# Second MLP of a hybrid decoder: seven products in all pairs of the seventh phase, its sums spread over the last phase, the last group of products in two halves

## The chip, the cores and the metric

The kernel runs on one core of one Trainium2 chip. The metric is the time of one execution on the device in microseconds (us); less is better. TensorE (PE) multiplies, VectorE (DVE) and ScalarE (ACT) work on tiles, GpSimd (POOL) and SyncE (SP) mostly issue DMA transfers. Each engine takes its own instructions in a fixed order; semaphores tie the engines together.

## The reference, cut to what matters

The reference is two layers of a decoder on 256 tokens and 16 leading meta tokens, width 2048, in float32: an RWKV-7 mixer, an MLP, a gated linear attention (GLA) with 4 heads, and a second MLP, each behind an RMS norm and added to its input. At the end stands a final RMS norm with a gain, and the meta tokens are dropped.

```
def rms_norm(x, g, eps=NORM_EPS):
    y = xf * lax.rsqrt(jnp.mean(xf * xf, axis=-1, keepdims=True) + eps)
    return y * g

def sq_relu_mlp(x, w1, w2):
    h = jax.nn.relu(x @ w1)
    return (h * h) @ w2          # w1: 2048 x 8192, w2: 8192 x 2048
```

The change concerns the second MLP's product with w2, the sum of that product with the residual, and the final norm. Other parts of the program are touched only where they prepare data for it.

## The kernel before, in words

The span has five stages, one after the other: the RWKV mixer (to some 592 us), the first MLP (function `mlp`, to some 1305), the GLA (`gla`, to some 1690), its output product, and the second MLP (`mlp1`, to the end at 2337).

**Weights.** TensorE works on float32 numbers as pairs of reduced-precision parts. A weight tile is loaded as `raw` by SyncE's queue; ScalarE casts it to `hi` (line 149 or 664), VectorE subtracts to get `lo` (line 150, or line 372 by way of the helper `tt`), and TensorE makes three matmuls of each product: with hi, with lo, with hi (lines 498 to 500 in `mlp1`; 172 to 174 in the other stages).

**The second MLP.** The 8192 hidden units are cut into 4 blocks b of 16 rows of 128; two rows make a pair p. The product with w2 is made in units (b, g, p), where g is a half of the 2048 outputs. `PHASES` gives the order of the eight phases (b, g); a phase has 8 pairs. The hidden rows of the next block (`row`, the product with w1, 16 ordinary matmuls for each of two stream entries) are woven between the pairs, except in the last phase.

An ordinary pair is a 2 by 2 block product with 8 products (24 matmuls of 128 x 512) from two weight tiles. A "fast" pair is the same product in Winograd's form with 7 products (21 matmuls) from three weight tiles A, B and E and a half tile G, which VectorE makes by subtracting a half of B from a half of A (`raw4`, in `split`, behind the lo of B). The slots A, B, E and G write PSUM banks 1 and 2, 6 and 7, 5 and 3, and 4. `FAST = [8, 8, 8, 4]` says how many pairs of each block are fast: all eight in blocks 0 to 2, four in block 3. Fast pairs use hidden blocks `HS` in 7 combinations (128 x 128 each, made by `sums` and `halves`), ordinary ones 4.

After a stretch of phases that share g, the banks are emptied and combined into `htok`, the residual in token layout: plain sums (`add`) and scaled sums (`into`, line 493), spread over later slots by `later(slot, f)`. The list `rest` has those for a stretch in which all pairs are fast (`alone`). The four steps on banks that ScalarE empties (`nc.scalar.mul`, `nc.scalar.copy`) are put behind the casts of their slot.

**The last phase**, (3, 1), takes its pairs in the order 0, 1, 4, 2, 3, 5, 6, 7: four fast ones, four ordinary ones. In phase (3, 0) of before, pairs 0 to 3 are fast and 4 to 7 ordinary, and its sums go to the first slots of the last phase. The last two pairs "close": the two products of token half 1 (banks 2 and 3) are made first, then its norm; then the 12 matmuls of one product of half 0 (`spare`, bank 0), then the 12 of the other (bank 4), then the norm of half 0. `final` squares a quarter of a token half and sums it (line 479), `most` adds these sums, `norm` makes the scale by two activations (lines 606, 607), scales (612, 613) and stores. `gain(t)` multiplies half the outputs of token half t by the gain `nf` ahead of that.

**What sets the order.** `mlp1` runs under a manual schedule on PE, DVE, ACT and SP: the order is that of the loop at its end. At stream entry i it issues what `later` put there (`before`), then the cast and the lo of entries up to four tiles ahead (`SETS = 4`), then what `later` put behind the casts (`behind`), then the matmuls of entry i. There are five raw buffers, and two more from three entries behind the last row. GpSimd is not under that schedule.

**The differences.** Fast pairs need differences of w2's quarters (tile `diff` in DRAM). `differences` makes them ahead of the second MLP, one unit (b, g, p) at a time: `fetch` (line 344: three loads of 256 KB by GpSimd's queue), `form` (lines 350 to 352: three VectorE operations, behind a small GpSimd copy in line 349), `store` (line 358). A step forms the unit fetched `delay` steps earlier, and stores the one before. `ticks` spreads the steps over rows of a stage. The first `EARLY = 52` units are made in the first MLP, with delay 2, the other 4 in the GLA, with delay 1, over 12 products: in the GLA the steps are at the ends of products 2, 4, 6, 8, 10 and 12, six products in each head.

## Time and profile before

| | us |
|---|---|
| median of 3 runs | 2339.42 |
| lowest and highest | 2338.92, 2340.03 |
| the profiled execution | 2338.97 |
| its span (first to last instruction) | 2337.2 |
| TensorE busy | 2308.0 (99% of the span) |
| VectorE busy | 1816.0 (78%) |
| ScalarE busy | 1378.0 (59%) |
| GpSimd busy | 301.4 (13%) |

A row of a timeline reads: start in us, duration in us, engine, line, operation, out<-in by the program's names, then the shape; `xN` is the number of instructions that the row stands for. In square brackets stands how long the engine was idle before it, and what released it. Matmuls are pipelined, so a row's duration is longer than the distance to the next one; the distance is the price. A tile is named by its first letters: `lo`, `hi`, `raw`, `HS`, `htok`; PSUM banks are `pu` (1, 2), `pt` (7, 6), `pm` (5), `pry` (3) and `pj` (4, 0).

### The profile page before, as it was taken

The page shows a single profiled execution, that of the slowest core. Times are in us where ns is not written, and L with a number is a line of the kernel's source. Part 1 is how long each engine was busy: PE and PEld are TensorE (multiplying, and loading weights), DVE is VectorE, ACT ScalarE, POOL GpSimd, SP SyncE. Part 2 cuts the span into 40 slices and gives each one's busy share as a digit, 9 for nine tenths or more (in the row PEclk, how much of TensorE's full clock was granted, in tenths as well). Part 3 has the DMA queues.
Part 4 walks back from the last instruction along what each step waited for, and adds up shares of the span by engine and source line. Part 5 has one row for each costly group of instructions (what it writes and reads, how often), then busy time and mean ns, then how long its engine had stood idle before and what let it go on. Part 6 is the DMA issues. An engine that isn't in the chain of part 4 may idle for free.

```text
span 2337.2 us, 49049 instructions
## 1 busy us (share of the span) xinstructions
PE 2308.0 (99%) x19183; PEld 2175.8 (93%) x19183; DVE 1816.0 (78%) x2979; ACT 1378.0 (59%) x2167; POOL 301.4 (13%) x597
## 2 busy tenths in 40 slices
PE   9999999999999999999999999999999999999998
PEld 8888888889999999999999999999998888898987
DVE  8868986848677667767767787677768989989877
ACT  6488645556555445445445565455577777777766
POOL 0000000000144444444430011000000000000000
PEclk9999999999999999999999999999999999999999
DMA  6459754535799999999996665555557777877875
GB/s 213 161 193 310 246 169 141 153 90 172 257 314 334 314 318 325 325 323 320 330 319 227 198 227 199 175 174 182 209 196 263 272 271 265 274 266 265 274 267 188
DMA packets 200326, 567.75 MB, mean 243 GB/s; under 512 B 41184, under 2 KB 56800, under 8 KB 199968
## 3 DMA queue, kind: packets, MB, share of 16 engines
q1 hardware_dynamic: 173216, 476.53, 59.7%
q0 software_dynamic: 26880, 88.10, 12.1%
q8 instruction: 151, 2.47, 0.4%
q14 instruction: 79, 0.65, 0.1%
HBM read 504.38 MB, written 58.46 MB: 241 GB/s over the span
## 4 chain that ended last, share of the span: by engine, by line
PE 83%; DVE 10%; ACT 3%; issue 2%; DMA 1%; SPq 0%; DVEq 0%; ACTq 0%
PE pj L172 16%; PE pj L174 16%; PE pj L173 16%; PE pj L418 10%; PE pj L419 5%; PE pj L205 2%; DVE lo L150 2%; PE pj L206 1%; PE pu L498 1%; PE pu L500 1%; PE pu L499 1%; PE pt L500 1%; PE pt L498 1%; PE pt L499 1%; ACT hi L149 1%
## 5 line engine op out<-in xcount | busy, mean ns | idle before, releaser
L149 ACT CAST hi<-raw 128x1024 fp32r<-128x1024 f32 (+1 forms) x562 | 526.1, 947 | 593.9 <-PE pj L173 530.6
L150 DVE TENSOR_TENSOR lo<-raw,hi 128x1024 fp32r<-128x1024 f32 (+1 forms) x562 | 613.1, 1100 | 224.8 <-ACT hi L149 220.1
L172 PE MATMUL pj<-x,hi 128*128 128x272 f32 (+1 forms) x2560 | 728.4, 285 | 2.0 <-DVE r L703 0.9
L174 PE MATMUL pj<-x,lo 128*128 128x272 f32 (+1 forms) x2560 | 714.7, 279 | 4.4 <-DVE lo L150 4.1
L173 PE MATMUL pj<-x,hi 128*128 128x272 f32 (+1 forms) x2560 | 713.6, 279 | 0.0
L172 PEld LDWEIGHTS pj<-x,hi 128*128 128x128 f32 x2560 | 484.8, 189 | 14.8 <-issue 6.5
L174 PEld LDWEIGHTS pj<-x,lo 128*128 128x128 f32 x2560 | 484.9, 189 | 6.8 <-DVE lo L150 6.5
L173 PEld LDWEIGHTS pj<-x,hi 128*128 128x128 f32 x2560 | 485.0, 189 | 2.5 <-issue 1.4
L372 DVE TENSOR_TENSOR lo<-raw,hi 128x1024 fp32r<-128x1024 f32 x364 | 405.1, 1140 | 72.1 <-ACT hi L664 70.8
L664 ACT CAST hi<-raw 128x1024 fp32r<-128x1024 f32 x364 | 352.3, 981 | 112.6 <-PE pj L418 30.7
L418 PE MATMUL pj<-x,hi 128*128 128x512 f32 x1024 | 339.5, 383 | 0.0
L172 PE MATMUL pj<-h,hi 128*128 128x272 f32 x1024 | 285.7, 279 | 0.0
L173 PE MATMUL pj<-h,hi 128*128 128x272 f32 x1024 | 285.7, 279 | 0.0
L174 PE MATMUL pj<-h,lo 128*128 128x272 f32 x1024 | 285.7, 279 | 0.0
L419 PE MATMUL pj<-x,lo 128*128 128x256 f32 x1024 | 279.2, 273 | 0.0
L418 PEld LDWEIGHTS pj<-x,hi 128*128 128x128 f32 x1024 | 193.5, 189 | 26.7
L419 PEld LDWEIGHTS pj<-x,lo 128*128 128x128 f32 x1024 | 196.4, 192 | 1.9 <-DVE lo L372 0.2
L172 PEld LDWEIGHTS pj<-h,hi 128*128 128x128 f32 x1024 | 193.5, 189 | 0.0
L173 PEld LDWEIGHTS pj<-h,hi 128*128 128x128 f32 x1024 | 193.5, 189 | 0.0
L174 PEld LDWEIGHTS pj<-h,lo 128*128 128x128 f32 x1024 | 193.5, 189 | 0.0
L358 POOL DMA_DIRECT2D diff<-x x168 | 90.2, 543 | 14.3 <-DVE x L351 5.1
L344 POOL DMA_DIRECT2D x<-w_d x168 | 89.8, 540 | 0.3
(359 smaller groups left out, 3517.7 us busy)
## 6 DMA issues: line engine op xcount, KB each, us to landing
raw<-mlp_w_d SPq DMA_DIRECT2D x384, 512.0 KB, 6.1
raw<-gla_in_d SPq DMA_DIRECT2D x98, 512.0 KB, 3.3
x<-w_d POOLq DMA_DIRECT2D x168, 256.0 KB, 6.8
diff<-x POOLq DMA_DIRECT2D x168, 256.0 KB, 8.6
raw<-w_rkv_d SPq DMA_DIRECT2D x80, 512.0 KB, 3.9
raw<-w_d SPq DMA_DIRECT2D x69, 512.0 KB, 4.5
raw<-diff SPq DMA_DIRECT2D x55, 512.0 KB, 5.2
raw<-gla_o_d SPq DMA_DIRECT2D x32, 512.0 KB, 3.3
```

Source lines behind the costliest of these rows:

```text
L149: nc.scalar.copy(hi[:, h], raw[:, h])
L150: nc.vector.tensor_tensor(out=lo[:, h], in0=raw[:, h], in1=hi[:, h].bitcast(F32), op=ALU.subtract)
L172: nc.tensor.matmul(out, hi[:, ws], xh, start=first, stop=False)
L173: nc.tensor.matmul(out, hi[:, ws], xl, start=False, stop=False)
L174: nc.tensor.matmul(out, lo[:, ws], xh, start=False, stop=last)
L205: nc.tensor.matmul(wide, hi[:, ws], xt, start=kt == 0, stop=False)
L344: nc.gpsimd.dma_start(x[:, body], w[:, k])
L358: nc.gpsimd.dma_start(self.diff[b, g, i][:, k], x[:, body])
L372: tt = lambda o, a, b, op: nc.vector.tensor_tensor(out=o, in0=a, in1=b, op=op)
L418: nc.tensor.matmul(wide, hi[:, ws], xt, start=kt == 0, stop=False)
L419: nc.tensor.matmul(narrow, lo[:, ws], xt[:, 0], start=False, stop=kt == KT - 1)
L664: nc.scalar.copy(hi, raw)
```

## The change

`FAST` becomes a table by phase: phase (3, 0) has eight fast pairs, phase (3, 1) still four. So 60 units need differences instead of 56, of which 54 are made in the first MLP and 6 in the GLA. Pairs 4 to 7 of block 3 are now fast in one phase and ordinary in the other; the one hidden block that only the ordinary form needs goes to a tile `X`. The sums of phase (3, 0) are those of an `alone` stretch, and `rest` is put at slots 8 to 14 behind its last tile, with the squares behind them. `gain(0)` moves from the ordinary pairs of the last phase to behind the norm of token half 1. The last product is made as two halves of 256 columns, in banks 4 and 1, with a squared sum for each half. The load of `nf` moves from SyncE's queue early in phase (3, 0) to GpSimd's queue at entry 12 of the last phase. `raw4` and `fsq` have one buffer instead of two.

```diff
-FAST = [8, 8, 8, 4]
+FAST = {phase: 8 for phase in PHASES}
+FAST[3, 1] = 4
 
-EARLY = 52
+EARLY = 54
...
-                if p >= FAST[b]:
-                    halves(slot + 1 + wait, F[:, :4], 0, 4)
-                    return
+                if p >= FAST[b, 1]:
+                    fourths[p] = X = self.t(hp, [P, 2, P], "X", KT // 2 - FAST[3, 1], F32R)
+                    later(slot + 2 + wait, lambda: nc.scalar.copy(X[:, 0], x21), True)
+                    later(slot + 3 + wait, lambda: tt(X[:, 1], x21, X[:, 0].bitcast(F32), ALU.subtract))
...
                                 for n, f in enumerate(rest):
-                                    later(slot + 7 + 2 * n, f)
+                                    later(slot + (7 + 2 * n if b < NHB - 1 else (8, 10, 10, 11, 11, 12, 14)[n]), f)
+                                if b == NHB - 1:
+                                    for n in range(4):
+                                        later(slot + 16 - n // 2 * 4, lambda n=n: final(n // 2, n % 2))
...
-                        if end and p == FAST[b] and k == 0:
-                            later(slot + 1, lambda: gain(0))
                         for at in (2, 3, 4, spare):
...
                         norm(1)
-                        for at in (spare, 4):
-                            for n, (X, m, pair) in enumerate(closing):
-                                h, ws = places[at][2:]
-                                product(at, (X[:, 0, 2 * m + h], X[:, 1, 2 * m + h]), pair, ws, False, n == 3)
-                            empty(at)
-                            if at == spare:
-                                most(0)
+                        gain(0)
+                        h, ws = places[spare][2:]
+                        for n, (X, pair) in enumerate(closing):
+                            product(spare, X[h], pair, ws, False, n == 3)
+                        empty(spare)
+                        most(0, (0, 1, 3))
+                        h, ws = places[4][2:]
+                        for i, at in enumerate((4, 1)):
+                            for n, (X, pair) in enumerate(closing):
+                                product(at, X[h], pair, ws, i == 1 and n == 0, n == 3, slice(P * i, P * i + P))
+                            into(0, 0, own[at], slice(SEQ * i, 512))
+                            final(0, 2 * g, i)
+                            if i == 0:
+                                add(sum3[:, :1], sum3[:, :1], ssq[:, 0, 4:])
+                                mean(0)
                         norm(0)
...
-            if n == len(PHASES) - 2:
-                gains_at = len(stream)
+            if n == len(PHASES) - 1:
+                gains_at = len(stream) + 12
...
-                    nc.sync.dma_start(nf, ap["nf"].to_broadcast([P, D]))
+                    nc.gpsimd.dma_start(nf, ap["nf"].to_broadcast([P, D]))
```

The order of instructions at three places follows, on VectorE; numbers behind a name are those of its buffer. Lines are those of each kernel, so that line 372 of before is 373 of the change. First the passage from phase (3, 0) to the last phase; `lo` is a weight tile's low part, `raw_4…` a half tile, `hres_72` the place of the sums u2, u3 and so on, `htok` the residual. Before:

```order
L372 TENSOR_TENSOR lo_28574<-raw_28468,hi_28573 128x1024
L372 TENSOR_TENSOR lo_28590<-raw_28488,hi_28589 128x1024
L372 TENSOR_TENSOR raw_4451_28593<-raw_28468,raw_28488 128x512
L372 TENSOR_TENSOR lo_28613<-raw_28506,hi_28612 128x1024
L372 TENSOR_TENSOR lo_4458_28619<-raw_4451_28593,hi_4457_28618 128x512
L372 TENSOR_TENSOR lo_28640<-raw_28529,hi_28639 128x1024
L493 SCALAR_TENSOR_TENSOR htok_22567<-pm_22575,rs_3273_22570,htok_22567 128x512
L372 TENSOR_TENSOR lo_28652<-raw_28555,hi_28651 128x1024
```

And with the change, at the first fast pair of the last phase as well:

```order
L373 TENSOR_TENSOR lo_28704<-raw_28596,hi_28703 128x1024
L373 TENSOR_TENSOR lo_28722<-raw_28621,hi_28721 128x1024
L373 TENSOR_TENSOR raw_4487_28725<-raw_28596,raw_28621 128x512
L373 TENSOR_TENSOR hres_72<-pt_22632,hres_72 128x512
L373 TENSOR_TENSOR hres_72<-pt_22631,hres_72 128x512
L373 TENSOR_TENSOR lo_28741<-raw_28672,hi_28740 128x1024
L373 TENSOR_TENSOR lo_4494_28747<-raw_4487_28725,hi_4493_28746 128x512
L373 TENSOR_TENSOR lo_28758<-raw_28675,hi_28757 128x1024
L373 TENSOR_TENSOR hres_72<-pm_22633,hres_72 128x512
L496 SCALAR_TENSOR_TENSOR htok_22625<-pm_22633,rs_3279_22628,htok_22625 128x512
L373 TENSOR_TENSOR lo_28775<-raw_28691,hi_28774 128x1024
```

Three plain sums, two of them from banks 6 and 7 (`pt`), now stand between the weight tiles of the first fast pairs, beside the scaled sum from bank 5 (`pm`) that stood there before.

Second, GLA's first head, at the end of its first product of values; `vs` is that product, `Am` a score block, `x` a unit of w2 that is formed, `lo` the next weight tile. What an instruction waits for stands in brackets; DMASW are GpSimd's transfers. Before:

```order
L1491 TENSOR_TENSOR vs_18026<-pj_17965,acc_17543 128x272 [waits PE_49]
L1491 TENSOR_TENSOR Am_18033<-pt_18028,gc_17552 80x256 [waits PE_49]
L150 TENSOR_TENSOR lo_18197<-raw_18194,hi_18196 128x1024 [waits DMAHW2_49,Activation_49]
L1491 TENSOR_TENSOR A_17960<-Am_18033,A_17960 80x256 [waits Activation_49]
L1491 TENSOR_TENSOR Am_18044<-pt_18037,gc_17552 128x192 [waits PE_49]
L1491 TENSOR_TENSOR Am_18051<-pt_18048,gc_17552 128x64 [waits DVE_49,PE_49]
```

And with the change:

```order
L1500 TENSOR_TENSOR vs_18058<-pj_17997,acc_17575 128x272 [waits PE_49]
L351 TENSOR_TENSOR x_17720<-x_17720,x_17719 128x513 [waits DMASW6_49,DMASW5_49,Pool_49]
L151 TENSOR_TENSOR lo_18229<-raw_18226,hi_18228 128x1024 [waits DMAHW2_49,Activation_49]
L352 TENSOR_TENSOR x_17719<-x_17719,x_17718 128x512 [waits DMASW4_49,DVE_49]
L1500 TENSOR_TENSOR Am_18075<-pt_18070,gc_17584 80x256 [waits PE_49]
L353 TENSOR_TENSOR x_17718<-x_17718,x_17720 128x512 [waits DVE_49]
L1500 TENSOR_TENSOR A_17992<-Am_18075,A_17992 80x256 [waits Activation_49]
L1500 TENSOR_TENSOR Am_18086<-pt_18079,gc_17584 128x192 [waits PE_49]
L1500 TENSOR_TENSOR Am_18093<-pt_18090,gc_17584 128x64 [waits DVE_49,PE_49]
```

The form of a unit (L351 to L353), which waits for the transfers of its fetch, now stands ahead of the first score block. On TensorE the third score block, `pt_18090`, which waits for VectorE to have read `pt_18070`, moves from behind the other scores to behind the 16th matmul of the next product. The steps with eight in all are at the ends of products 2, 3, 5, 6, 8, 9, 11 and 12; the same passage comes again in the second head at product 9.

Third, the end of the program; `pj_…` are banks 0 and 4, `pu` is bank 1, `sum` the sum of squares, `ssq` its parts, `rt` the norm's scale. Before:

```order
L612 SCALAR_TENSOR_TENSOR htok_22567<-htok_22567,rt_4520_28937,hres_72 128x512 x2
L493 SCALAR_TENSOR_TENSOR htok_22567<-pj_22578,rs_3273_22570,htok_22567 128x512
L372 TENSOR_TENSOR sum_3272_22569<-ssq_22568 128x1
L372 TENSOR_TENSOR sum_3272_22569<-sum_3272_22569,ssq_22568 128x1
L602 TENSOR_SCALAR sum_3272_22569<-sum_3272_22569 128x1
L493 SCALAR_TENSOR_TENSOR htok_22567<-pj_22577,rs_3273_22570,htok_22567 128x512
L612 SCALAR_TENSOR_TENSOR htok_22567<-htok_22567,rt_4523_28981,hres_72 128x512 x2
```

And with the change:

```order
L621 SCALAR_TENSOR_TENSOR htok_22625<-htok_22625,rt_4554_29063,hres_72 128x512 x2
L373 TENSOR_TENSOR htok_22625<-htok_22625,hres_72 128x1024
L496 SCALAR_TENSOR_TENSOR htok_22625<-pj_22636,rs_3279_22628,htok_22625 128x512
L373 TENSOR_TENSOR sum_3278_22627<-ssq_22626 128x1
L373 TENSOR_TENSOR sum_3278_22627<-sum_3278_22627,ssq_22626 128x1
L496 SCALAR_TENSOR_TENSOR htok_22625<-pj_22635,rs_3279_22628,htok_22625 128x512
L373 TENSOR_TENSOR sum_3278_22627<-sum_3278_22627,ssq_22626 128x1
L611 TENSOR_SCALAR sum_3278_22627<-sum_3278_22627 128x1
L496 SCALAR_TENSOR_TENSOR htok_22625<-pu_22629,rs_3279_22628,htok_22625 128x256
L621 SCALAR_TENSOR_TENSOR htok_22625<-htok_22625,rt_4558_29124,hres_72 128x512 x2
```

The gain of token half 0 (128x1024) has come in behind the norm of half 1; bank 4 (`pj_22635`) is emptied over all its 512 columns first, since it also holds earlier pairs' products, then come a third sum and the mean, and then the 256 columns of bank 1.

More of the change, by code (lines that the diff above doesn't have):

```diff
@@ L332, in differences @@
         if not hasattr(self, "diff"):
-            self.diff = self.t(self.dp, [NHB, 2, max(FAST), P, 3, 512], "diff")
-        units = [(b, g, i) for b, g in PHASES for i in range(FAST[b])][part]
+            self.diff = self.t(self.dp, [NHB, 2, KT // 2, P, 3, 512], "diff")
+        units = [(b, g, i) for b, g in PHASES for i in range(FAST[b, g])][part]
         held = {}
@@ L483, in unit @@
             w = self.operands(b, g, p)
-            phase = PHASES.index((b, g))
+            phase, fast = PHASES.index((b, g)), FAST[b, g]
             opens = phase == 0 or PHASES[phase - 1][1] != g
@@ L500, in product @@
                 nc.tensor.matmul(o, X[1], wh, start=False, stop=stop)
-            if p < FAST[b]:
+            if p < fast:
                 def pe(todo):
@@ L543, in unit, with blocks, ordinary @@
             places = {2: (1, 0, 1, one), 3: (1, 1, 1, two), spare: (0, 1, 0, two), 4: (0, 0, 0, one)}
-            def ordinary(at, H, k, w, stop):
+            def blocks(k, h):
+                H, i = hid[p], 2 * k + h - 1
+                return (fourths[p][:, 0], fourths[p][:, 1]) if i < 0 else (H[:, 0, i], H[:, 1, i])
+            def ordinary(at, k, w, stop):
                 h, ws = places[at][2:]
-                product(at, (H[:, 0, 2 * k + h], H[:, 1, 2 * k + h]), w, ws, at == spare and p == FAST[b] and k == 0, stop)
+                product(at, blocks(k, h), w, ws, at == spare and p == fast and k == 0, stop)
             def empty(at):
@@ L575, in run @@
                     for at in (2, 3):
-                        ordinary(at, H, k, w, last and k == 1)
+                        ordinary(at, k, w, last and k == 1)
                     if last and k == 1:
@@ L1727, in _blocks @@
     for b in range(NHB):
-        out[b, :, : FAST[b]] = w[b, :, : FAST[b]][..., [0, 2, 3, 1], :]
+        for g in range(2):
+            n = FAST[b, g]
+            out[b, g, :n] = w[b, g, :n][..., [0, 2, 3, 1], :]
     return out
```

59 lines of the change are left out of this document (26 added, 33 removed).

## The prediction

> **What bounds the kernel now.** I read the page first, then the table of windows for the stages that the change touches, then the timelines of TensorE (PE), VectorE (DVE), ScalarE (ACT) and GpSimd (POOL) there. The page:
>
> ```profile
> PE 2308.0 (99%) x19183; PEld 2175.8 (93%) x19183; DVE 1816.0 (78%) x2979; ACT 1378.0 (59%) x2167; POOL 301.4 (13%) x597
> ```
>
> TensorE is the bound for the whole span. So work taken from it counts in full, and work given to another engine costs only where TensorE comes to wait for it. The stages (the columns are PE, PEld, DVE, ACT, POOL busy, granted clock, DMA share, GB/s):
>
> ```profile
> 600.00:1250.00 650.00, 650.00 (x5614) 650.00 (x5613) 458.82 (x582) 296.15 (x373) 269.61 (x520) 1.00 0.92 316
> 1333.00:1407.00 74.00, 74.00 (x652) 73.20 (x651) 59.31 (x125) 42.25 (x78) 13.24 (x29) 1.00 0.69 230
> 2290.40:2321.10 30.70, 30.23 (x141) 26.19 (x139) 30.59 (x37) 20.92 (x29) 0.00 (x0) 1.00 0.65 227
> ```
>
> Row 1 is the first MLP, row 2 the first head of GLA, row 3 the last phase of the second MLP. In the last, VectorE is busy for 30.59 of 30.70 us: it already works without a pause, and is just in time. That is the stage into which the change moves sums.
>
> **The change, part by part.** *Four pairs lose a product each.* The rate of TensorE in these phases:
>
> ```profile
> 2287.93 0.38 PE L498 MATMUL pu<-hi,HS 128*128 128x512 f32 x1
> 2290.30 0.38 PE L500 MATMUL pt<-hi,HS 128*128 128x512 f32 x1
> 2291.15 0.48 PE L498 MATMUL pm<-hi,HS 128*128 128x512 f32 x1 [0.47 <-DVE htok L493]
> 2291.47 0.38 PE L499 MATMUL pm<-lo,HS 128*128 128x512 f32 x1
> ```
>
> From the first to the second row are 11 intervals, so one matmul takes 2.37/11 = 0.2155 us. A pair with eight products has 24 of them, one with seven 21; four pairs save 12 x 0.2155 = **-2.6 us**. Rows 3 and 4 show what before pays for its own sums: 2290.30 to 2291.15 is 0.85 instead of 0.22, and 0.32 instead of 0.22 follows, 0.7 us in all.
>
> *Sums spread over the last phase.* VectorE takes its queue strictly in order here. Its prices, from start to start where rows touch:
>
> ```profile
> 2292.15 0.69 DVE L372 TENSOR_TENSOR raw<-raw,raw 128x512 f32<-128x512 f32 x1
> 2292.75 2.96 DVE L372 TENSOR_TENSOR lo<-raw,hi 128x1024 fp32r<-128x1024 f32 x3
> 2316.16 1.41 DVE L493 SCALAR_TENSOR_TENSOR htok<-hres,rs,htok 128x512 f32<-128x512 f32 x2
> 2317.49 1.22 DVE L372 TENSOR_TENSOR lo<-raw,hi 128x1024 fp32r<-128x1024 f32 x1
> 2319.94 1.23 DVE L372 TENSOR_TENSOR lo<-raw,hi 128x1024 fp32r<-128x1024 f32 x1
> 2321.08 1.23 DVE L372 TENSOR_TENSOR htok<-htok,hres 128x1024 f32<-128x1024 f32 x1
> ```
>
> An operation on 512 columns takes 0.60 (2292.15 to 2292.75), one on 1024 columns 1.14 (2319.94 to 2321.08), a scaled sum 0.665 (1.33 for two). A fast pair costs VectorE three weight tiles and two half tiles, 3 x 1.135 + 2 x 0.60 = 4.61 us, against 21 x 0.2155 = 4.53 of TensorE: nothing is left for sums. An ordinary pair costs 2.27 against 5.17. How far VectorE is ahead when the last pair of the seventh phase starts is read where before has the same thing, a fast pair without a row behind fast pairs with rows (the end of the fifth phase):
>
> ```profile
> 2123.54 1.22 DVE L372 TENSOR_TENSOR lo<-raw,hi 128x1024 fp32r<-128x1024 f32 x1
> 2123.97 0.38 PE L498 MATMUL pu<-hi,HS 128*128 128x512 f32 x1
> 2126.01 0.48 PE L500 MATMUL pt<-hi,HS 128*128 128x512 f32 x1 [0.15 <-DVE HS L372]
> ```
>
> VectorE starts on the second weight tile of the pair 0.43 us before TensorE starts the pair, and TensorE already has to wait 0.15 in it. From there to the last weight tile of the kernel VectorE now has 22 tiles (24.97), ten half tiles of five fast pairs (6.0), the last hidden blocks (0.8), the seventh phase's sums (six plain, five scaled: 6.9) and the last phase's (three and five: 5.1), together 43.8; with about 1.0 of waits on ScalarE and banks, less the 0.43, it ends 44.4 us after TensorE's start of that pair. TensorE's work up to the split that needs this tile is 21 + 4 x 21 + 2 x 24 + 12 + 6 + 1 = 172 matmuls, 37.07 us. So it is held for 7.4 us, mostly at the first fast pairs of the last phase (whose banks the sums must empty first: some 4.6 together) and at the last two splits (2.2). Before's 0.7 goes: **+6.7 us**. If VectorE comes in with the 2.3 us of two more tiles done, the hold is 5.1 and the term 4.4. ScalarE's casts (20.92 us busy in that row) and the four more weight loads (at a DMA share of 0.65) run beside this and add nothing.
>
> *The tail.* Here is before's end:
>
> ```profile
> 2326.31 0.75 DVE L493 SCALAR_TENSOR_TENSOR htok<-pj,rs,htok 128x512 f32<-128x512 f32 x1
> 2327.09 0.63 ACT L479 ACTIVATE fsq<-htok 128x512 f32<-128x512 f32 x1 [0.78 <-DVE htok L493]
> 2327.37 0.38 PE L500 MATMUL pj<-hi,HS 128*128 128x512 f32 x1
> 2327.84 0.16 DVE L372 TENSOR_TENSOR sum<-sum,ssq 128x1 f32<-128x1 f32 x1 [0.72 <-ACT fsq L479]
> 2328.03 0.15 DVE L602 TENSOR_SCALAR sum<-sum 128x1 f32<-128x1 f32 x1
> 2328.11 0.74 DVE L493 SCALAR_TENSOR_TENSOR htok<-pj,rs,htok 128x512 f32<-128x512 f32 x1
> 2328.88 0.63 ACT L479 ACTIVATE fsq<-htok 128x512 f32<-128x512 f32 x1 [1.07 <-DVE htok L493]
> 2329.63 0.29 ACT L606 ACTIVATE rt<-ssq,sum 128x1 f32<-128x1 f32 x1
> 2330.20 1.41 DVE L612 SCALAR_TENSOR_TENSOR htok<-htok,rt,hres 128x512 f32<-128x512 f32 x2 [1.35 <-ACT rt L607]
> ```
>
> TensorE is done by 2327.75, but VectorE empties the last bank only at 2328.11, behind its own chain; the last norm follows 2.09 later. The change puts the 1024-column gain of token half 0 into that chain, ahead of the emptying at 2326.31: +1.14. The last product in two halves makes the chain longer as well, since the first half's sum now stands before the second half's emptying: the first emptying, still 512 columns wide, 0.77 (2328.11 to 2328.88), its square 0.53 (0.75 from 2328.88 to 2329.63, less 0.22 for half the columns), sum and mean 0.27 (2327.84 to 2328.11); the second emptying 0.47 (half the columns), its square 0.53, and 0.57 to the scaling. That is 3.14 instead of 2.09, less the 0.19 that the mean took ahead of the emptying before: +0.86. Together **+2.0**. If TensorE is so late that VectorE waits for it instead, the halves save that wait and the columns of the second emptying and square, 0.36 + 0.33 + 0.21 = 0.9: the bounds are -0.9 and +2.0.
>
> *Differences: two more units in the first MLP, two more in GLA.* A unit is fetched by three transfers of 256 KB on GpSimd's queue, formed by three VectorE operations, and stored. In the first MLP VectorE has 191 us to spare (row 1 of the windows), and nothing there waits on these: 0. In GLA the steps fall closer: with eight steps over twelve products, unit 0 is formed one product after its fetch, where before it was two, and so unit 4 in the second head. These forms stand in VectorE's queue ahead of a score block that TensorE waits for. GpSimd's fetches in the two heads, with landing times, and all twelve:
>
> ```profile
> L344 POOL DMA_DIRECT2D x<-w_d x3: 536/541/541, 1334.0 to 1335.1; - x3
> DMA to landing us min/median/max: 5.7/7.4/8.3
> ...
> L344 POOL DMA_DIRECT2D x<-w_d x3: 536/541/541, 1408.5 to 1409.5; - x3
> DMA to landing us min/median/max: 6.0/6.2/6.3
> ...
> DMA to landing us min/median/max: 5.5/6.2/8.3
> ```
>
> And TensorE and VectorE at the place:
>
> ```profile
> 1337.02 2.83 PE L1602 MATMUL pt<-Q,KX 128*80 128x64 f32 x24
> 1338.16 0.42 DVE L1491 TENSOR_TENSOR Am<-pt,gc 80x256 f32<-80x256 f32 x1 [0.49 <-PE pt L1602]
> 1339.66 0.36 PE L172 MATMUL pj<-x,hi 128*128 128x272 f32 x1
> 1341.02 0.28 PE L174 MATMUL pj<-x,lo 128*128 128x272 f32 x1
> 1412.43 0.42 DVE L1491 TENSOR_TENSOR Am<-pt,gc 80x256 f32<-80x256 f32 x1 [0.18 <-PE pt L1602]
> ```
>
> In head 0 the last fetch, issued at 1335.1, lands at 1343.4. Then come the first operation of the form, a weight tile, the second, and the block Am: 0.60 + 1.14 + 0.60 + 0.42 and 0.1 of handing over, 2.85; TensorE can have its bank at 1346.25. It wants it after 16 matmuls of the next product: twelve of them start between 1339.66 and 1341.02, the other four take 0.5 more, and the last score block, moved behind them, takes some 0.3 off ahead, so at 1341.2. Held: 5.1 us. In head 1, 74.3 later by the two Am rows, it wants it at 1415.5; the fetch lands at 1409.5 + 6.2 = 1415.7, and the bank comes free at 1418.6: 3.1 us. That is 8.2 at most; with the fastest landing, 5.5, in both it is 2.3 + 2.3 = 4.6. I take **+7.5**, near the upper end, since the landings of these very fetches give that one.
>
> The gain vector's load moves from SyncE's queue, early in the seventh phase, to GpSimd's in the last. Before's issue and landing:
>
> ```profile
> L697 SPq DMA_DIRECT2D hres<-nf_d x1: 382/382/382, 2216.0 to 2216.0; - x1
> DMA to landing us min/median/max: 7.5/7.5/7.5
> ```
>
> Its first reader now stands 60 matmuls of TensorE after the issue's slot, 13 us, and GpSimd has nothing else in that window (0.00 in the third row of the windows), so 7.5 or 8.3 are covered. If that cover is gone, the gain of token half 1 waits for it, with the last weight tiles queued behind, at us per us.
>
> *At nothing:* single buffers for the half tile and the squares (their readers stand earlier in the same queues); the separate tile for one hidden block (0.4 of VectorE, in pairs with rows).
>
> **Sum.** -2.6 + 6.7 + 2.0 + 7.5 = +13.6 on the profiled execution's 2338.97: 2352.6. The median of the runs lies 0.45 above that execution, so 2353.0. From the bounds, 2344.9 (4.4, -0.9, 4.6) to 2354.0 (6.7, 2.0, 8.2, and 0.3 for a load that lands late).
>
> **Rivals.**
>
> *The fetch is there in time.* If the transfers land within 3.1 us (1335.1 to the Am at 1338.16), the closer steps in GLA cost nothing: -2.6 + 6.7 + 2.0 = +6.1, 2345.5 as a median. Against it stand twelve landings of 5.5 us and more; for it only that the queues may be emptier after the change moves the steps. The Trainium skill, on its page "DMA: Bandwidth & Descriptors" in the section "Anatomy of one DMA — SWDGE (gpsimd) path", fits 2.0 us plus the bytes at 436 GB/s to a transfer of GpSimd; for 256 KB that is an estimate of 2.6 us, and by it this rival would be the forecast. The trace does not agree: 5.5 to 8.3 us. 17%.
>
> *VectorE's queue never reaches TensorE (the other side).* VectorE has 14.7 us idle in the GLA window; if it comes into the last phase with more than some 7 us of tiles done, and finds the forms' data landed, only the removed matmuls, a remnant of 0.5 and the tail count: -2.6 + 0.5 and -0.9 to +2.0, so 2336.4 to 2339.3, not slower. The point from which this decides is VectorE's lead at the first fast pair of the last phase. Against it: 30.59 of 30.70 us busy there with fewer sums, and a lead of 0.43 us at the like place. 13%.
>
> *A third form holds too.* Unit 2 is also formed one product after its fetch. I count nothing for it, since a whole product lies between. If it costs what head 1's does, 3.1 more: 2356.1. 10%.
>
> **Numbers.** The forecast has 60%, at 2353.0. The range, 2344 to 2357, takes in its bounds, the first rival and the third; it leaves out the second and the lower edge of the first. A measurement of this kernel can tell about 0.2%, 4.7 us, from no change, so "same" is 2334.7 to 2344.1: most of the second rival (10%) and 4% of the first; 3% are faster; the rest, 83%, is slower.
>
> **What would show it.** In the changed kernel's trace: TensorE idle for some 5 us at the 17th matmul of the first head's second product, and some 3 at the same place in head 1, ended by VectorE's Am; idle times summing to 7 in the last phase, at the second product of the first fast pair, at the first matmul into pm of it, and at the last two splits; VectorE busy without a pause from the last pair of the seventh phase to the last tile; the last norm's scaling some 2 us later against TensorE's end than before. The prediction is wrong if VectorE shows idle time in the last phase, or if the forms in GLA start without waiting for a DMA.

## The result and the profile after

The changed kernel takes 2362.92 us (median of 4 runs, 2362.3 to 2364.26) against 2339.73 of the kernel before (4 runs, 2338.92 to 2340.45): ratio 1.01, 95% interval 1.0082 to 1.0117. It is 23.2 us slower, where 13.6 were forecast (2353.0), and outside the range. The page, engines busy:

```profile
PE 2317.5 (98%) x19183; PEld 2182.4 (92%) x19183; DVE 1837.1 (78%) x3025; ACT 1385.6 (59%) x2182; POOL 319.3 (14%) x638
```

To see where the time went, both traces are cut at the same events: the first score block of the GLA, the first matmul of the second MLP on its hidden blocks, the last weight tile's low part on VectorE, the end. The table of windows, before:

```profile
1337.00:1747.05 410.05, 409.94 (x3237) 395.46 (x3236) 305.91 (x565) 238.21 (x412) 17.52 (x34) 1.00 0.57 194
1747.05:2319.94 572.89, 571.97 (x3063) 511.37 (x3062) 507.87 (x636) 417.93 (x565) 0.00 (x0) 1.00 0.78 265
2319.94:2337.19 17.25, 7.81 (x36) 6.35 (x34) 8.59 (x17) 6.49 (x16) 0.00 (x0) 0.79 0.37 122
```

And after:

```profile
1338.68:1765.09 426.41, 416.75 (x3237) 401.37 (x3235) 309.33 (x571) 237.98 (x412) 23.99 (x55) 0.98 0.58 194
1765.09:2342.21 577.12, 573.11 (x3057) 510.88 (x3055) 520.26 (x668) 425.48 (x578) 0.54 (x1) 1.00 0.79 267
2342.21:2361.37 19.16, 6.99 (x43) 5.97 (x41) 10.26 (x20) 6.87 (x18) 0.00 (x0) 0.83 0.33 109
```

The second number of a row is the stretch's length. The stretch with the GLA is 16.4 us longer, the second MLP 4.2, the tail 1.9, and the 1.7 at the left are there before the GLA. As much is lost in the mixer, where the two programs are the same: TensorE waits there for VectorE for 1.9 us in both, at 301 us, but only in the changed kernel's execution is the clock halved behind it, for 3.41 us. The same stretch, before:

```profile
300.00:310.00 10.00, 8.23 (x77) 7.64 (x77) 9.53 (x21) 2.56 (x5) 0.00 (x0) 1.00 0.66 194
```

And after; the number behind the five busy times is the granted clock:

```profile
303.54:306.95 3.41, 3.41 (x24) 3.19 (x23) 3.38 (x8) 0.00 (x0) 0.00 (x0) 0.50 0.72 216
306.95:310.36 3.41, 3.41 (x31) 3.41 (x30) 2.33 (x4) 1.14 (x2) 0.00 (x0) 1.00 0.82 211
```

In the table, the granted clock of the first row after is 0.98, where it was 1.00: that is the one number in these rows that the prediction had no term for. Close up, the first head, TensorE:

```profile
1342.69 0.28 PE L173 MATMUL pj<-x,hi 128*128 128x272 f32 x1
1348.28 1.12 PE L1611 MATMUL pt<-Q,KX 128*128 128x64 f32 x4 [5.31 <-DVE Am L1500]
...
1349.97 0.43 PE L174 MATMUL pj<-x,hi 128*128 128x272 f32 x1
1350.20 0.43 PE L175 MATMUL pj<-x,lo 128*128 128x272 f32 x1
...
1355.09 0.28 PE L173 MATMUL pj<-x,hi 128*128 128x272 f32 x1
1355.21 0.28 PE L174 MATMUL pj<-x,hi 128*128 128x272 f32 x1
```

VectorE at the same place, and GpSimd's fetch with its landings:

```profile
1345.46 0.70 DVE L351 TENSOR_TENSOR x<-x,x 128x513 f32<-128x513 f32 x1 [6.14 <-DMA x<-w_d]
...
1347.81 0.41 DVE L1500 TENSOR_TENSOR Am<-pt,gc 80x256 f32<-80x256 f32 x1
```

```profile
L345 POOL DMA_DIRECT2D x<-w_d x3: 538/543/543, 1334.9 to 1338.6; - x3
...
DMA to landing us min/median/max: 4.9/5.8/6.8
```

This is the forecast wait, with the forecast chain: the transfer lands, VectorE forms, a weight tile stands between, Am follows, TensorE goes on. It holds TensorE for 5.5 us (1342.69 to 1348.28, less one interval). What follows it was not forecast: from 1348.3 to 1354.6 two matmuls start 0.23 us apart (1349.97 and 1350.20), then 0.12 again (1355.09 and 1355.21). The windows give the clock beside it:

```profile
1344.00:1348.00 4.00, 0.00 (x0) 0.00 (x0) 2.54 (x4) 0.00 (x0) 0.55 (x1) 1.00 0.53 202
1348.00:1354.00 6.00, 5.72 (x28) 5.36 (x29) 3.76 (x10) 2.39 (x6) 1.09 (x2) 0.50 0.57 192
1356.00:1390.00 34.00, 33.03 (x289) 32.20 (x288) 25.04 (x43) 19.03 (x38) 8.91 (x20) 1.00 0.69 235
```

Behind the wait TensorE runs at half its clock for 6.3 us, so 3.1 us of work are lost. The second head has the same: a wait of 3.4 us, and 3.1 behind it. A third wait, 1.2 us at the end of the first head (the prediction's third rival), leaves the clock alone. Together 5.5 + 3.4 + 1.2 = 10.1 of waits and 6.2 of half clock, 16.3 of the 16.4.

The last phase, from the first fast pair's neighbourhood to the last splits, TensorE's waits and the window:

```profile
PE pu L501 <- ACT hres L517: 2.2, 1, 2.2
PE pu L502 <- DVE lo L373: 1.7, 2, 0.9
...
PE pt L503 <- DVE HS L373: 0.3, 1, 0.3
PE pm L501 <- DVE htok L496: 0.2, 1, 0.2
```

```profile
2299.00:2343.00 44.00, 40.00 (x172) 32.74 (x170) 43.23 (x53) 28.91 (x39) 0.54 (x1) 0.96 0.68 241
```

VectorE is busy for 43.23 of 44 us. And the end, VectorE:

```profile
2348.66 1.22 DVE L373 TENSOR_TENSOR htok<-htok,hres 128x1024 f32<-128x1024 f32 x1
2349.79 0.74 DVE L496 SCALAR_TENSOR_TENSOR htok<-pj,rs,htok 128x512 f32<-128x512 f32 x1
...
2352.98 0.15 DVE L611 TENSOR_SCALAR sum<-sum 128x1 f32<-128x1 f32 x1
2353.05 0.47 DVE L496 SCALAR_TENSOR_TENSOR htok<-pu,rs,htok 128x256 f32<-128x256 f32 x1
2354.72 1.41 DVE L621 SCALAR_TENSOR_TENSOR htok<-htok,rt,hres 128x512 f32<-128x512 f32 x2 [1.20 <-ACT rt L616]
```

From the first emptying of half 0 to the scaling are 4.93 us (2349.79 to 2354.72), where before had 3.89 (2326.31 to 2330.20), and the gain's 1.14 stands ahead.

### The profile page after: what moved, and what is told of

It is laid out like the page before. It is cut to its first block, busy times and chain, and to the rows that moved or that the text cites. A ratio compares the mean times of both kernels' runs of the same rounds, so it can differ in the third digit from the quotient of the medians.

```text
span 2361.4 us, 49213 instructions
## 1 busy us (share of the span) xinstructions
PE 2317.5 (98%) x19183; PEld 2182.4 (92%) x19183; DVE 1837.1 (78%) x3025; ACT 1385.6 (59%) x2182; POOL 319.3 (14%) x638
## 4 chain that ended last, share of the span: by engine, by line
PE 81%; DVE 12%; ACT 3%; issue 2%; DMA 2%; POOL 0%; SPq 0%; DVEq 0%; ACTq 0%; POOLq 0%
PE pj L173 16%; PE pj L175 15%; PE pj L174 15%; PE pj L419 9%; PE pj L420 5%; PE pj L206 2%; DVE lo L151 2%; PE pj L207 1%; PE pt L503 1%; DVE upd L712 1%; PE pt L501 1%; PE pt L502 1%; DVE lo L373 1%; PE pu L501 1%; PE pu L502 1%
## 5 line engine op out<-in xcount | busy, mean ns | idle before, releaser
L373 DVE TENSOR_TENSOR lo<-raw,hi 128x1024 fp32r<-128x1024 f32 x371 | 410.3, 1133 | 66.8 <-ACT hi L673 66.1
L673 ACT CAST hi<-raw 128x1024 fp32r<-128x1024 f32 x371 | 357.3, 978 | 108.2 <-PE pj L419 30.4
L359 POOL DMA_DIRECT2D diff<-x x180 | 97.1, 545 | 24.5 <-DVE x L351 10.4
```

The source lines that it names most:

```text
L359: nc.gpsimd.dma_start(self.diff[b, g, i][:, k], x[:, body])
L373: tt = lambda o, a, b, op: nc.vector.tensor_tensor(out=o, in0=a, in1=b, op=op)
L673: nc.scalar.copy(hi, raw)
```

## The experiments

Theory: the waits in the GLA come from the distance between fetch and form; a long wait also costs half the clock for some microseconds; the last phase's loss comes from VectorE's queue; the tail's from the gain and the halves. Rivals are named in each expectation. All times are medians, and a wait is the distance of two starts of matmuls less one interval, where nothing else is said; the kernel before took 2340.2 to 2340.6 beside these runs.

**e1, 56 units in the first MLP.**

```diff
-EARLY = 54
+EARLY = 56
```

> The changed kernel with 56 units of differences made in the first MLP, so that the GLA makes 4 again, at before's steps; the last phases are untouched. Theory: the loss has two places. In the GLA the forms hold TensorE for 5.5, 1.2 and 3.4 us, and after the two long holds TensorE runs at half its clock for some 6 us, which costs 3.1 us each time: 16.4 in all. The other 6.3 are in the last phase. So 2362.9 - 16.4 = 2346.5, within 1.5, and no wait of TensorE in the GLA. Rival A (two more units of differences cost the first MLP something, or most of the loss is in the last phase and the GLA's part is only moved): above 2350. Rival B (the 1.9 us that the two traces differ by before the first MLP comes from the change): it stays in the trace of this run; by the theory it is the spread of runs.

Measured: 2347.91 (2345.51 to 2349.56, 6 runs), 15 us less than the change. The GLA's stretch, cut at the same events, is before's:

```profile
1338.09:1748.12 410.03, 409.92 (x3237) 395.45 (x3236) 305.81 (x565) 238.33 (x412) 17.57 (x34) 1.00 0.59 194
```

So the GLA's loss is the two more units, whole, and rival A falls. The remaining ratio, 1.0032 (1.002 to 1.0045), is the last phases. Rival B falls too: the 1.9 us are mostly the halved clock in the mixer, which this trace does not have. The GLA starts 1.1 us later here than in before's, in the traces below from 0.6 earlier to 3.8 later: that is the spread of executions. In the last phase of this trace the clock is halved for 6.8 us (from 2289.84), twice as long as in the change's.

**e2, the same steps in the kernel before.**

```diff
-EARLY = 52
+EARLY = 50
```

> The kernel before with 50 units of differences made in the first MLP and 6 in the GLA, so that the GLA's steps are those of the change, and nothing else of the change is there. Theory: holds and half clock as in the change: +16.4 on 2339.7, 2356, within 1.5. Rival (only the waits count, and the low clock behind them is hidden, as TensorE would wait for VectorE again anyway): +10.1, 2350. Rival (the holds need something else of the change): 2340.

Measured: 2353.68 (4 runs), ratio 1.0057 (1.0042 to 1.0072), 13.5 more than before, between the two forecasts. The trace has both parts:

```profile
PE pt L1602 <- DVE Am L1491: 6.4, 2, 3.6
PE pu L1615 <- DVE Vl L1491: 0.7, 1, 0.7
```

```profile
1346.00:1352.00 6.00, 5.91 (x31) 5.54 (x32) 3.72 (x10) 2.39 (x6) 1.09 (x2) 0.55 0.55 181
```

The GLA's stretch is 13.4 us longer than before's. The waits are shorter here than in the change (3.8, 0.9 and 3.0, 7.6 in all; the landings differ from run to run), and the half clock behind the two long ones, for 5.3 and 6.5 us, takes the other 5.8. So it is not hidden, and the GLA's loss needs nothing else of the change.

**e3, matmuls in the wait.**

```diff
+                    if s == 1 and hd < 2:
+                        warm = self.pm()
+                        for i in range((64, 46)[hd]):
+                            nc.tensor.matmul(warm[:, :SEQ], x[0][:, 0, :P], x[1][:, 0, :SEQ], start=True, stop=True)
```

> The changed kernel with matmuls on data at hand, into a bank that nobody reads, put where TensorE waits for the third score block: 64 of 128x256 in the first head and 46 in the second, some 7 and 5 us. The score block comes right behind them, so the 16 matmuls that stood ahead of the wait now stand behind it and cost 1.86 us in each head. Theory (after a long hold the clock is halved for some 6 us, and it is idle time of TensorE that halves it): granted clock 1.00 behind the waits, and 3.1 - 1.86 = 1.25 us less in each head: 2362.9 - 2.5 = 2360.4. Rival (the low clock has another cause, or TensorE's pace there is set by VectorE and not by the clock): 2 x 1.86 more, 2366.6.

Measured: 2365.8, but wide: 2361.28 in the profiled execution, 2365.1 to 2366.8 in the other three. On the clock the trace is clear. The windows of the filled wait and of what follows, first head, then second:

```profile
1339.00:1347.00 8.00, 8.00 (x70) 8.00 (x69) 3.27 (x5) 0.41 (x1) 2.13 (x4) 1.00 0.74 262
1347.00:1353.00 6.00, 5.49 (x45) 5.02 (x45) 2.21 (x9) 2.28 (x5) 0.55 (x2) 1.00 0.43 163
1423.00:1428.00 5.00, 5.00 (x44) 5.00 (x44) 2.78 (x5) 0.00 (x0) 1.56 (x4) 1.00 0.99 388
1428.00:1434.00 6.00, 5.68 (x48) 5.21 (x47) 2.55 (x8) 2.39 (x6) 1.03 (x2) 1.00 0.76 306
```

With TensorE kept busy the clock stays at 1.00 in this execution: it is the idle time that halves it. The heads get only 0.35 and 0.15 us shorter than in the change, not 1.25, since the fill ended behind the data. On the time the experiment decides nothing: the profiled execution is near the theory's 2360.4, the median near the rival's 2366.6, and why three executions took 4 us more is open.

**e4, six units, formed two steps behind the fetch.**

```diff
-        left, oT = [[... for _ in range(3)] for _ in range(3)], []
-        tick = self.ticks(self.differences(slice(EARLY, None), lambda u: left[u % 3], 1), 12)
+        left, oT = [[... for _ in range(3)] for _ in range(4)], []
+        tick = self.ticks(self.differences(slice(EARLY, None), lambda u: left[u % 4], 2), 12)
```

> The changed kernel, still with 6 units made in the GLA, but each formed two steps behind its fetch instead of one, with a fourth set of tiles. The forms then stand behind the score blocks in VectorE's queue. Theory (the distance between fetch and form makes the holds, not the number of units): no holds of over 1 us, no low clock in the GLA, 2346.5 as for the first of these runs, within 1.5. Rival (six units are too many for VectorE or the DMA queues there, wherever they stand): holds stay, above 2352.

Measured: 2353.42 (4 runs), ratio 1.0053 (1.0038 to 1.0068). The theory's time is missed by 6.9 us, and the rival's "above 2352" is met. In the trace the three waits of the change are gone, so the distance made them. But a new one has come, at the scores of the second head:

```profile
PE pt L1611 <- DVE KX L1590: 3.0, 1, 3.0
```

VectorE makes KX late there because its queue stands behind a weight tile, whose cast waits on ScalarE for a load of the GLA's own weights:

```profile
1412.25 1.05 ACT L150 CAST hi<-raw 128x1024 fp32r<-128x1024 f32 x1 [5.50 <-DMA raw<-gla_in_d]
1413.33 1.22 DVE L151 TENSOR_TENSOR lo<-raw,hi 128x1024 fp32r<-128x1024 f32 x1 [3.29 <-ACT hi L150]
```

The clock is halved behind this wait for 3.4 us, and the GLA's stretch is 4.9 us over before's instead of 16.4. One more wait, 1.6 us for VectorE, stands ahead of that stretch. So the rival has this much in it: with six units something else came late here. Whether their transfers delayed that load is not shown.

**e5, the price of a wait by itself.** A program of its own:

```
for n, steps in SECTIONS:
    for _ in range(n):
        nc.tensor.matmul(bank, w, hi, start=True, stop=True)
    nc.vector.tensor_tensor(out=t, in0=raw[:, 0, 512:1024], in1=bank, op=ALU.min)
    for _ in range(steps):
        nc.vector.tensor_tensor(out=t, in0=t, in1=raw[:, 0, 512:1024], op=ALU.max)
    nc.vector.tensor_tensor(out=w, in0=t[:, :P], in1=raw[:, 1, :P], op=ALU.max)
```

> A program of its own that leaves out the whole computation: sections of 61 to 75 matmuls of 128x512, and after each TensorE waits for VectorE, which takes the bank, makes 0 to 14 operations of 0.6 us one after the other, and writes the weights of the next section. It measures what a wait costs beyond itself. Theory: a wait shorter than some 2 us leaves the clock at 1.00; one of 3.4 us and more always halves it behind the wait, for about 6 us, which costs 3 us; between them it depends on where the wait falls (in the runs so far waits of 1.2, 2.48 and 2.68 us left it, waits of 2.41 and 2.99 halved it). The Trainium skill, on its page TensorE: Matmul & The Clock Gate in Part 1, says that a free-running window of about 3.4 us decides. Rival: the clock falls in proportion to the wait, or only behind waits that follow other ones.

Measured, from the starts of its matmuls, which lie 0.227 us apart at full clock (a matmul counts as slow when the next starts over 0.3 us later):

| wait, us | halved, of so many waits | extra time behind it when halved |
|---|---|---|
| 1.27 | 0 of 2 | |
| 1.99 | 1 of 5 | 1.8 |
| 2.72 | 3 of 5 | 1.6 to 1.7 |
| 3.45 | 3 of 5 | 1.6 to 2.7 |
| 4.17 to 11.44 | 12 of 12 | 1.7 to 2.5 |

Where it is not halved, the first matmuls behind a wait take 0.15 more, which is in the last column too. One of the waits of 4.17 us, and what follows:

```profile
105.60:109.50 3.90, 0.15 (x1) 0.00 (x0) 3.54 (x6) 0.00 (x0) 0.00 (x0) 1.00 0.00 0
109.60:114.00 4.40, 4.24 (x12) 3.35 (x13) 0.11 (x1) 0.00 (x0) 0.00 (x0) 0.65 0.00 0
```

The price does not grow with the wait: the halving is there or not, and behind the wait it lasts 3.3 to 5.6 us here, so the first rival falls. The theory holds in kind but not in its numbers: one wait of 1.99 us halved the clock, two of 3.45 left it, and a halving cost 1.6 to 2.7 instead of 3. The second rival is not excluded by the table: the first four waits of the program, 1.27 to 3.45 us, left the clock at 1.00.

The times at which the granted clock changes in the 13 traces kept for this case show what decides. In each trace all halved stretches begin on one grid of 3.41 us and last one to four of its steps; only the last, behind the end of TensorE's work, is cut short. Of 109 waits of over 1 us (from 60 us on; in e5 all), 26 have more than 2.1 us inside one step, and behind all of them the clock is halved; 71 have less than 1.9 inside any step, and behind none of them it is; of the 12 between, 5 halved it. That also accounts for the first four waits, which have at most 2.1 inside a step, so the second rival falls. A wait of over 4.2 us has more than 2.1 inside one step wherever it falls. The grid lies differently to the program in each execution, and so a wait of 2 to 4 us halves the clock or not by chance, as the 1.9 us in the mixer did in 3 of 12 traces.

**e7 and e8, the two parts of the tail,** both on e1's kernel.

```diff
                         mean(1)
+                        gain(0)
                         norm(1)
-                        gain(0)
```

> The changed kernel with 56 units made in the first MLP (as in the first experiment) and the gain of token half 0 ahead of the scaling of half 1, in the time in which VectorE waits for that norm's scale (0.93 us idle in the changed kernel's trace). Theory (the gain's 1.14 us in VectorE's last chain are half of the tail's loss): from VectorE's last weight tile to the end 18.1 us instead of 19.16, and the whole about 1.0 under the first experiment's 2347.9, 2346.9. Rival (TensorE or the stores set the end): 19.1 and no change.

```diff
+                        mean(0)
                         h, ws = places[4][2:]
-                        for i, at in enumerate((4, 1)):
...
+                        for n, (X, pair) in enumerate(closing):
+                            product(4, X[h], pair, ws, False, n == 3)
+                        empty(4)
```

> The same base with the last product undivided, as before: one emptying, one square, the mean ahead of it; the gain stays late. Theory (the halves make VectorE's last chain longer, since TensorE has been done for long): 0.86 less, 18.3 from the last weight tile to the end, 2347.0. Rival (the halves hide a half of the emptying behind TensorE, as they could if TensorE ended last): longer by up to 0.5, 19.7, 2348.4.

Measured: 2345.35 and 2345.32 (10 runs each), both 1.002 of before (1.001 to 1.0029). From VectorE's last weight tile to the end 18.14 and 18.20 us, against 19.16: 1.0 and 1.0, as forecast. So the gain and the halves cost about the same. In e7 the gain stands where VectorE waited, and the norm follows without idle time:

```profile
2329.18 1.21 DVE L373 TENSOR_TENSOR htok<-htok,hres 128x1024 f32<-128x1024 f32 x1
2330.31 1.41 DVE L621 SCALAR_TENSOR_TENSOR htok<-htok,rt,hres 128x512 f32<-128x512 f32 x2
```

The medians fell by 2.6, more than that, but the intervals overlap e1's; the windows from the last weight tile are what shows the 1.0. A part of the rest may be e1's longer half clock in the last phase, which neither of these two traces has.

**e9, eight operations on GpSimd,** on e1's kernel.

```diff
...
+                                        rest[n] = lambda c=c, x=x: nc.gpsimd.tensor_tensor(out=c, in0=c, in1=x, op=ALU.add)
...
-                tt(fourth[g], raws[i - 1][:, two], raw[:, two], ALU.subtract)
+                sub = nc.gpsimd if i > rows_end else nc.vector
+                sub.tensor_tensor(out=fourth[g], in0=raws[i - 1][:, two], in1=raw[:, two], op=ALU.subtract)
```

> The same base with the half tiles of the seventh phase's last pair and of the last phase, and the three plain sums of the seventh phase that need no bank, on GpSimd instead of VectorE: 8 operations of 0.60, 4.8 us off VectorE's queue between the last pair's start and the last weight tile. Theory (VectorE's queue, 44.4 us against 37.1 of TensorE, makes the holds of the last phase): TensorE's holds there fall from 7.6 to about 2.8, and the time to 2347.9 - 4.8 = 2343.1. If GpSimd is slower than 1.5 us an operation, or slows VectorE beside it, part of that is lost, and its latency shows as a wait for raw4. Rival (the loads of differences or ScalarE make the holds): no change, 2347.9.

Measured: 2348.2 (7 runs), no gain. It does not speak against the theory, since VectorE's time did not fall. GpSimd, and two weight tiles of VectorE, the first beside it and the second not:

```profile
2310.97 1.94 POOL L683 TENSOR_TENSOR raw<-raw,F 128x512 f32<-128x512 f32 x1
```

```profile
2311.69 2.29 DVE L373 TENSOR_TENSOR lo<-F,hi 128x1024 fp32r<-128x1024 f32 x1
...
2314.57 1.21 DVE L373 TENSOR_TENSOR lo<-F,hi 128x1024 fp32r<-128x1024 f32 x1
```

What VectorE gave away came back as longer operations: from the start of the seventh phase's last pair to the last split it is busy for 45.0 us, where it is 44.0 in e7 and e8. TensorE's 172 matmuls there take 9.0 us over their intervals instead of 7.7 in e7 and e8.

**e10, three fast pairs in the last phase, and both tail edits.**

```diff
-FAST[3, 1] = 4
+FAST[3, 1] = 3
...
-EARLY = 54
+EARLY = 55
...
-            for p in range(KT // 2) if more or not second else (0, 1, 4, 2, 3, 5, 6, 7):
+            for p in range(KT // 2) if more or not second else (0, 1, 3, 4, 2, 5, 6, 7):
...
```

> The changed kernel with three fast pairs in the last phase instead of four (pair 3 ordinary, order 0, 1, 3, 4, 2, 5, 6, 7), 55 units in the first MLP and 4 in the GLA, the gain of half 0 ahead of the norm of half 1, and the last product undivided; the squares' unread output is in bf16 to make room. The base is the changed kernel with 56 units, 2346.8 by the three kernels run on it so far (2347.9; 2345.35 + 1.0; 2345.32 + 0.9). Theory (VectorE's queue against TensorE's work): a pair less costs TensorE 0.65 and gives VectorE 2.34; the holds at the first fast pair stay, about 5.2 with the one ahead of it, and the two at the last splits (2.2) go; the tail gives 1.9 back. -2.2 + 0.65 - 1.9: 2343.3. Rival (the holds at the last splits come from something else, the loads or ScalarE): they stay, and the time is 2345.6.

Measured: 2343.82 (10 runs), ratio 1.0013 (1.0003 to 1.0022), as forecast within 0.5. The holds at the last splits have gone from the list; the early ones stay:

```profile
PE pu L501 <- ACT hres L517: 2.3, 1, 2.3
PE pt L503 <- DVE HS L373: 0.4, 1, 0.4
PE pm L501 <- DVE htok L496: 0.2, 1, 0.2
```

**e11, without the spread sums,** on e1's kernel.

```diff
-                                for n, f in enumerate(rest):
+                                for n, f in enumerate(rest if b < NHB - 1 else []):
...
```

> The base (56 units in the first MLP, otherwise the changed kernel) without the three plain and four scaled sums of the seventh phase that are spread over slots 8 to 14: it leaves these out of the result, the sums that free the banks stay. Theory (VectorE's queue): 4.5 us less on VectorE, but only behind the holds at the first fast pair, which stay at about 5.2 with the one ahead of it; the two at the last splits (2.2) go, since VectorE is then 2.3 us ahead. 2346.8 - 2.2 = 2344.6. Rival (the spread sums also make the first holds): up to 4.5 less, 2342.3. Rival (they cost nothing): 2346.8.

Measured: 2346.92 (10 runs), and the 172 matmuls take 6.6 us over their intervals instead of 7.7. The early holds stay at 5.0 (0.5, 2.6, 1.9). Of the two late ones the first is gone, the second stays at 1.06: the last phase's own sums stand right ahead of the last weight tile. So the spread sums make only one of the late holds, 1.1 us, not 2.2. The time decides nothing at this size: it is 1.0 under e1's median and at the 2346.8 of the rival for which the sums cost nothing, and the profiled execution came to the GLA 2.0 later than before's, with the clock halved in the mixer as in the change's.

**e12, the scaling earlier,** on e1's kernel.

```diff
-                                later(slot + 2, lambda: nc.scalar.mul(v2, own[2], rs2[:, 1:2]), True)
+                                later(slot + (2 if b < NHB - 1 else 1), lambda: nc.scalar.mul(v2, own[2], rs2[:, 1:2]), True)
```

> The base with the scaling of bank 2 (v2, by ScalarE) one slot earlier, ahead of two casts of which the first waits for a load. In the changed kernel's trace TensorE's longest hold of the last phase, 2.4 us at the second product of the first fast pair, is ended by that scaling. Theory (VectorE, busy without a pause, sets the sum of the holds): that hold goes, and the next one, at the first matmul into pm, ended by VectorE's scaled sum, grows by as much; the sum stays at 7.6 and the time at 2346.8. Rival (ScalarE's late scaling is a cost of its own): 2.4 less, 2344.4.

Measured: 2349.91 (5 runs, 2347.01 to 2352.38), 2 to 3 more, where 0 or 2.4 less was expected; its interval overlaps e1's, so the trace has to tell. The trace, TensorE, and the clock behind it:

```profile
2292.40 0.48 PE L501 MATMUL pt<-hi,HS 128*128 128x512 f32 x1 [0.79 <-DVE hres L373]
...
2297.41 0.77 PE L501 MATMUL pm<-hi,HS 128*128 128x512 f32 x1 [3.31 <-DVE htok L496]
```

```profile
2297.40:2303.00 5.60, 5.59 (x13) 4.51 (x14) 4.57 (x5) 1.66 (x2) 0.00 (x0) 0.50 0.75 264
```

The wait for the scaling has gone and is found again at VectorE's sums, 0.95 and 3.47 us, as the theory has it. But two waits have become one long one, and the clock halved behind it for 5.6 us, with VectorE no longer late: some 2.8 us lost. The 172 matmuls take 47.8 us, where they take 44.8 in e7 and e8. In this execution, cutting a wait that another replaces made the kernel slower.

## Why the prediction was wrong, point by point

- *Four products less, -2.6, and the sums, +6.7.* Right: +4.1 forecast, +4.2 measured between the same events. The 172 matmuls of the sum, forecast at 37.07 us and 7.4 of holds, took 44.7. The holds stand where they were put: 0.5 at the pair ahead, 2.4 at the first fast pair's second product, 2.0 at the last two splits. At the first matmul into pm only 0.4 are left, because TensorE ran at half clock for 9 matmuls ahead of it (2.0 us more); VectorE set the pace there, so that cost nothing: in e3, e4, e7 and e8, with the clock at 1.00 in this stretch, the 172 matmuls took 44.8. In e1's trace, where the half clock lasted twice as long, they took 46.1, so there 1.3 us of it did cost. That VectorE's queue makes the sum is shown by e12 (a hold taken away comes back at VectorE) and e10 (2.34 us less of VectorE, and the late holds go). e11 corrects a detail: of the late holds, one belongs to the last phase's own sums.
- *The tail, +2.0.* Right: 1.9, half from the gain (e7), half from the halves (e8).
- *The differences in the GLA, +7.5.* This step failed. Its mechanism and its places are right (e1, e2), and its waits are not far off: 5.5 and 3.4 against 5.1 and 3.1. The third transfer of the first fetch was issued at 1338.6 rather than, with the stage's shift, at 1336.8, and landed in 6.8 instead of 8.3. The third form, a rival, held for 1.2. But the step took the price of a hold to be its length, and so came to 7.5 where 16.4 were measured. Each of the two long holds halved TensorE's clock behind it, 3.1 us more each, 6.2 that no term had. The Trainium skill says on its page "TensorE: Matmul & The Clock Gate", in Part 1, that the array's clock falls to half after an idle window of about 3.4 us, and that the window runs freely. The runs agree that a wait can halve the clock and that its place matters; with the numbers of e5, a wait of 1.99 us did it once in five, and one of 3.45 failed to in two of five. The runs do not bear out that a whole window must be idle: more than 2.1 us inside one step of 3.41 were enough each time (e5). The rows of before that the prediction used held no such wait, and their clock was 1.00. Elsewhere before's trace has one near that length, the 1.9 us in the mixer, and its clock stayed too, so it could not show the price.
- *At nothing.* Right: the first MLP took the same time, to 0.01 us between the same matmuls (695.00 us from 600.42 before and from 602.33 after), with two more units, and nf landed 7.1 us after its issue at 2326.1, ten ahead of its reader.
- *The rivals.* The landings were 4.9 to 7.9 us, so the fetch was not there in time; VectorE's queue did reach TensorE. The third form held, for 1.2 instead of 3.1: its first operation waited 3.1 us for its transfers, and the tile Vl that TensorE needs stood behind it on VectorE.
- *The rest of the difference:* 10.1 + 6.2 + 4.2 + 1.9 is 22.4 of the 23.2 between the medians; the 1.7 ahead of the GLA in the two traces are the halved clock in the mixer, which has nothing to do with the change.

No version here beats the kernel before. e10 comes nearest, at 1.0013. By VectorE's account it could not win: with three fast pairs VectorE still needs 44.4 - 2.34 = 42.1 us, against 37.07 + 0.65 = 37.7 of TensorE, so 4.4 us of holds stay wherever they are put, more than the 2.6 - 0.65 = 1.95 us of matmuls saved.

## What to carry to other kernels

A wait of the matmul engine has two prices: its length, and, from about 2 us on, a chance that the clock is halved for some 3 to 7 us behind it; above 4 us that was always so here. So count holds one by one, and prefer several short ones to a long one; but where another engine sets the pace, the low clock is free for as long as that engine is behind (2.0 us of it here). And an engine that is only just in time takes no more work: moving it to an engine that blocks the first one moves nothing.

## What the runs showed of the hardware that was not expected

- The halved clock as above: on a grid of 3.41 us, behind each of 26 waits with more than 2.1 us inside one step, behind none of 71 with less than 1.9.
- GpSimd and VectorE slow each other on tiles in SBUF: VectorE's 128x1024 subtraction took 2.29 us instead of 1.21 beside a GpSimd subtraction, and GpSimd's took from 1.27 to 3.31 us. The Trainium skill, on its page "SBUF — State Buffer" in the section "SBUF: two separate sides", calls the port pair of the two an exclusive lock and says that the loser blocks; these numbers agree with that, but do not show which of the two held the ports.
